# A two-block decoder on one core: the order of background steps on VectorE, ScalarE and GpSimd

## The chip, the core and the metric

The kernel runs on one core of one Trainium2 chip. The metric is the device time of one execution in microseconds; the median of three runs is given. The trace of one more execution on the same chip says what each engine did: TensorE (PE, with its weight loads PEld), VectorE (DVE), ScalarE (ACT), GpSimd (POOL) and SyncE (SP), whose queue issues nearly all DMAs.

## The reference

256 tokens of width 1024 pass through a first block of two layers and then a second block of one layer, all in float32. Cut to what matters:

```python
for l in range(2):
    x = x + 0.5 * swiglu(rms_norm(x, g1), w_gate, w_up, w_down)        # 1024 -> 2816 -> 1024
    pa, pb, pc, pd = split(rms_norm(x, gm) @ w_in)                     # 768, 416, 768, 512
    y = concat([neighbourhood(pa), mla(pb), differential(pc), gqa(pd)])
    x = x + y @ w_out
    x = x + 0.5 * swiglu(rms_norm(x, g2), ...)
    x = rms_norm(x, gf)
u = rms_norm(x) @ w_in_2                                               # second block
x = x + (ga * (pool(u) @ wa) + gb * (swa(u) @ wb) + gc * (moba(u) @ wc)) @ w_out_2
return rms_norm(x)
```

Each of the four mixers of a layer norms its heads (or its latents), forms scores, softmax and values for 256 queries and 256 keys, and norms its result. The weights are some 220 MB and are read once; the 256 tokens are two tiles of 128.

## The kernel before, in words

**Products.** A float32 product is made of three in the fast float32r form: every weight and every activation is held as a high part and a low part, and `acc` (line 339) adds high by high, high by low and low by high in PSUM. Activations are the stationary operand, weights the moving one, 512 columns wide.

**Weights.** `Weights` (from line 158) takes the weight matrices in one order, in units of 128 x 1024. `load` (line 183) starts the DMA of a unit into one of three staging buffers (`st`) from SP's queue. `cut` (line 194) makes the high part on ScalarE (`hi`, a copy to float32r) and the low part on VectorE (`lo`, a subtraction), into one of six pairs of buffers, and then starts the next load. A staging buffer is free when both have read it; a pair is free when the matmuls of its unit are done. `can_cut` (line 212) says whether the pair is free.

**Main line and background.** The main line is written out in order: gate, up and down products of a feed-forward net (`ffn`, line 546), the projections of the mixers (`proj`, line 496), the output projection (`wide`, line 521), and in the second block the same with gates. After each group of matmuls it calls `tick` (line 446), which resumes up to four background steps that are ready and emits one cut if it can. A background step is a Python generator put into a list by `spawn`: the chains of the four mixers (`differential` 928, `latent` 821 for the MLA heads, `neighbourhood` 960, `grouped` 977) with their head norms, `softmax_pv` (line 572, scores, softmax, transposes and values of one job after the other; one chain at a time may be in its scores) and the norm of the result (`post_rms`, line 765); in a feed-forward net the transposes of the hidden units (`trans_split`, line 394, spawned at line 562); at the start the second half of the first norm (lines 1093 to 1096); in the second block `moba` 1178, `swa` 1199, `pooling`, `silus` and `gated`. What is ready is decided by `Clock`, a small model of the engines' times that the kernel runs while it is traced. So the order of the program is this planner's. The main line's own work on other engines (evictions of a projection, updates of x, the norm of x between stages, the cuts) is not part of a step.

**From the program's order to the engines' queues.** The list scheduler of the language takes, for each engine, the instruction of lowest place among those that are ready; an instruction's place is its position in the program, counted over all engines. Every call on VectorE, ScalarE and GpSimd goes through `Engine` (line 125). There an instruction with an operand in PSUM is issued with `high_priority(14)`, which takes 14 off its place; others keep theirs. The two returns are the lines that the profile shows: L153 is an instruction issued ahead, L154 one that was not. TensorE's instructions (L333 matmuls, L337 transposes) and the DMAs always keep their places. Each engine then runs its queue in the order so found.

**Norms of heads.** `rpow` (line 348) makes the power -0.5 of several columns by a Newton iteration of eleven small instructions on VectorE (`ms`, `r`, then three times `q`, `q`, `r`), and of fewer than four columns by one instruction on GpSimd.

Of the kernel before, what the change touches and what calls it, by code (L numbers as in the profile page):

```python
# [39 lines left out]
FIRST = [1, 1, 2, 2, 2]  # L40
WARM = 6
AHEAD = 14
OUT_ORDER = (4, 5, 2, 3, 0, 1, 6, 7)
IN2 = {"ax": 0, "az": 512, "bq": 1024, "bkv": 1536, "bz": 1792,
       "cq": 2304, "ck": 2816, "cv": 3328, "cz": 3840, "g": 4352}
# [4 lines left out]
def _free(ap):  # L50
    n = 1
    for d in ap.shape[1:]:
        n *= d
    return n
# [6 lines left out]
class Clock:  # L61
# [3 lines left out]
    def __init__(self):  # L65
        self.t = {"pe": 0.0, "act": 0.0, "dve": 0.0, "pool": 0.0}
        self.last = 0.0
        self.writes, self.reads = {}, {}
        self.rings = {}

# [54 lines left out]
class Engine:  # L125
# [5 lines left out]
    def __getattr__(self, op):  # L131
        f = getattr(self._eng, op)

        def call(*args, **kw):
            aps = [v for v in list(args) + list(kw.values()) if isinstance(v, bass.AP)]
            outs = [kw["out"] if "out" in kw else args[0]]
            if "accum_out" in kw:
                outs.append(kw["accum_out"])
            ins = [v for v in aps if not any(v is o for o in outs)]
            n = max(_free(v) for v in [outs[0]] + ins[:1])  # L140
            sb = all(v.space != bass.MemoryType.PSUM for v in aps)
            if self.name == "act":
                cost = 55 + 0.84 * n + sum(93 for k in ("scale", "bias", "accum_out")
                                           if not isinstance(kw.get(k, 1.0), float))
            elif self.name == "dve":
                fast = sb and op in ("tensor_copy", "tensor_scalar")
                cost = 65 + (0.52 if fast else 1.04) * n
            else:
                cost = 300 + 165 * n if kw.get("op") == ALU.pow else 100 + 1.1 * n
            self._clock.op(self.name, cost, outs, ins)  # L150
            if not sb:
                with self._tc.high_priority(AHEAD):
                    return f(*args, **kw)  # L153
            return f(*args, **kw)  # L154
        return call
# [74 lines left out]
def decoder(ctx, tc, a, out):  # L230
    nc = tc.nc
    clock = Clock()
# [31 lines left out]
    for l in range(L):  # L264
        for f in (1, 2):
            if f == 2:
# [8 lines left out]
                ws.add(wi, 8, 512, 2, (OFF_GQA, OFF_GQA + 512))  # L275
                for k in OUT_ORDER:
                    ws.add(a["w_out"][l][k * 128:(k + 1) * 128, :], 1, D, 1)
# [143 lines left out]

    def resume(e):
        clock.last = e[2]
        try:
            d = next(e[0])
        except StopIteration:
            bg.remove(e)
            return
        e[2] = clock.last
        e[1] = d if callable(d) else clock.last if d is None else d  # L430

# [3 lines left out]
    def run_ready():  # L435
        for e in bg:
            if is_ready(e):
                resume(e)
                return True
        return False  # L440
# [12 lines left out]
    def drain_until(cond):  # L453

        while not cond():
            if not run_ready():
                e = min((e for e in bg if not callable(e[1])), key=lambda e: e[1])
                clock.wait_pe(e[1])
                resume(e)
# [61 lines left out]
    def wide(order, hi, lo, blocks, evac, before=None):  # L521


        nk = len(order)
        pss = [[psM() for _ in range(2)] for _ in range(2)]
        i0 = 0
        for b in blocks:
            w = [get() for _ in range(b)]
            last = i0 + b == nk
            for t in range(2):  # L530
                for hs in ((0,), (1,)) if last else ((0, 1),):
                    for i in range(i0, i0 + b):
                        k = order[i]
                        if before:
                            drain_until(lambda: before(k, t))
                        acc([(pss[t][h], h * 512, 512) for h in hs], hi[:, k, tok(t)],
                            lo[:, k, tok(t)], w[i - i0], 0, i == 0, i == nk - 1)
                        if t == 1 and hs[-1] == 1:
                            ws.end(w[i - i0])
                        if i < nk - 1:  # L540
                            tick()
                    if last:
                        evac(t, hs[0], pss[t][hs[0]])
            i0 += b
# [167 lines left out]
    def mixers(l, cols, rows, nlam, norm_out):  # L712
# [359 lines left out]
        def before(k, t):  # L1072
            k0 = k // 2 * 2
            return (k0, t) in finished and (k0 == 6 or (k0, 1) in finished)
        wide(OUT_ORDER, yTh, yTl, [1] * 4 + [4], lambda t, h, ps: norm_out.update(t, h, ps, 1.0),
             before)
# [367 lines left out]
```

## Time and profile before

| | |
|---|---|
| median of 3 runs | 1319.79 us (1315.48 to 1320.84) |
| the profiled execution | 1318.63 us |
| its span, first to last instruction | 1316.5 us |
| mean granted clock of TensorE | 0.995 |
| busy: PE, PEld | 98%, 79% |
| busy: DVE, ACT, POOL | 60%, 55%, 2% |

Times in the rows are microseconds, from the span's start. A matmul row counts as busy until its modelled end, and matmuls overlap; idle time stands in brackets behind a row with what ended it. The feed-forward nets and mixers follow one another: the first layer's mixers lie at about 205 to 345, the second layer's at about 715 to 865, the second block's attention at about 1085 to 1165.

### The profile page before, as it was taken

The page shows a single profiled execution, that of the slowest core. Times are in us where ns is not written, and L with a number is a line of the kernel's source. Part 1 is how long each engine was busy: PE and PEld are TensorE (multiplying, and loading weights), DVE is VectorE, ACT ScalarE, POOL GpSimd, SP SyncE. Part 2 cuts the span into 40 slices and gives each one's busy share as a digit, 9 for nine tenths or more (in the row PEclk, how much of TensorE's full clock was granted, in tenths as well). Part 3 has the DMA queues.
Part 4 walks back from the last instruction along what each step waited for, and adds up shares of the span by engine and source line. Part 5 has one row for each costly group of instructions (what it writes and reads, how often), then busy time and mean ns, then how long its engine had stood idle before and what let it go on. Part 6 is the DMA issues. An engine that isn't in the chain of part 4 may idle for free.

```text
span 1316.5 us, 17826 instructions
## 1 busy us (share of the span) xinstructions
PE 1291.3 (98%) x6514; PEld 1046.1 (79%) x6514; DVE 792.7 (60%) x1615; ACT 722.5 (55%) x1223; POOL 28.6 (2%) x44
## 2 busy tenths in 40 slices
PE   8999999999999999999999999999999999999997
PEld 7788888766788888788888876678888887678886
DVE  5655449895655544755545798565554565555475
ACT  6544437866644444644435676664444466566543
POOL 0000001000000000100000000000000000000000
PEclk9999999999999999999999998999999999999999
DMA  8766657432566665666665733156667474245652
GB/s 278 219 181 188 183 166 238 126 97 65 172 190 184 183 188 164 208 183 188 186 186 167 218 115 98 45 179 189 185 181 235 144 234 127 80 145 168 205 170 80
DMA packets 109815, 221.80 MB, mean 168 GB/s; under 512 B 7456, under 2 KB 30368, under 8 KB 109728
## 3 DMA queue, kind: packets, MB, share of 16 engines
q1 hardware_dynamic: 109152, 220.04, 55.5%
q8 instruction: 51, 0.84, 0.3%
q10 hardware_dynamic: 576, 0.63, 0.1%
q14 instruction: 36, 0.29, 0.1%
HBM read 219.59 MB, written 1.05 MB: 168 GB/s over the span
## 4 chain that ended last, share of the span: by engine, by line
PE 82%; DMA 6%; DVE 5%; ACT 4%; issue 1%; POOL 1%; SPq 0%; POOLq 0%; ACTq 0%; DVEq 0%
PE mmps L333 71%; PE tps L337 6%; PE sps L333 3%; DMA st<-in_w_in_dram 3%; PE tps L333 3%; DVE lo L154 2%; ACT hi L154 2%; DMA st<-in_ffn_w_gate_dram 2%; DMA st<-in_ffn_w_up_dram 1%; DVE xTl L153 1%; ACT junk L154 1%; ACT xTh L153 1%; POOL r L154 1%; DVE x L153 0%; DVE qkT L153 0%
## 5 line engine op out<-in xcount | busy, mean ns | idle before, releaser
L154 DVE TENSOR_TENSOR lo<-st,hi 128x1024 fp32r<-128x1024 f32 (+2 forms) x403 | 488.2, 1214 | 395.3 <-ACT hi L154 394.5
L154 ACT ACTIVATE hi<-st 128x1024 fp32r<-128x1024 f32 (+2 forms) x403 | 421.9, 1050 | 427.6 <-PE mmps L333 348.8
L333 PE MATMUL mmps<-hi,xTh 128*128 128x512 f32 (+2 forms) x1200 | 451.9, 377 | 1.0 <-ACT xTh L153 1.0
L333 PE MATMUL mmps<-hi,xTl 128*128 128x512 f32 (+2 forms) x1200 | 446.3, 372 | 0.0
L333 PE MATMUL mmps<-lo,xTh 128*128 128x512 f32 (+2 forms) x1200 | 446.2, 372 | 0.0
L333 PEld LDWEIGHTS mmps<-hi,xTh 128*128 128x128 f32 x1200 | 226.1, 188 | 42.4 <-issue 2.5
L333 PEld LDWEIGHTS mmps<-hi,xTl 128*128 128x128 f32 x1200 | 226.2, 188 | 38.2 <-issue 0.5
L333 PEld LDWEIGHTS mmps<-lo,xTh 128*128 128x128 f32 x1200 | 226.3, 189 | 36.2 <-issue 1.0
L333 PE MATMUL mmps<-lo,hTh 128*128 128x512 f32 x352 | 138.1, 392 | 0.0
L333 PE MATMUL mmps<-hi,hTh 128*128 128x512 f32 x352 | 137.8, 392 | 0.0
L333 PE MATMUL mmps<-hi,hTl 128*128 128x512 f32 x352 | 113.6, 389 | 0.0
L333 PE MATMUL mmps<-hi,yT 128*128 128x512 f32 (+1 forms) x248 | 89.0, 416 | 0.6 <-ACT yT L153 0.6
L333 PEld LDWEIGHTS mmps<-hi,hTl 128*128 128x128 f32 x352 | 66.1, 188 | 13.6
L333 PEld LDWEIGHTS mmps<-hi,hTh 128*128 128x128 f32 x352 | 66.1, 188 | 13.6
L333 PEld LDWEIGHTS mmps<-lo,hTh 128*128 128x128 f32 x352 | 66.1, 188 | 13.1
L154 POOL TENSOR_TENSOR r<-ms,mhalf 128x1 f32<-128x1 f32 x40 | 28.4, 711 | 1283.1 <-DVE ms L154 1283.0
L333 PEld LDWEIGHTS mmps<-hi,yT 128*128 128x128 f32 x248 | 46.1, 190 | 11.4 <-ACT yT L153 1.9
L333 PE MATMUL mmps<-lo,yT 128*128 128x512 f32 (+1 forms) x124 | 49.7, 401 | 0.0
L154 ACT ACTIVATE E<-E,nm 128x256 f32<-128x256 f32 (+1 forms) x80 | 38.3, 480 | 14.9 <-DVE nm L154 14.7
L153 ACT ACTIVATE fg<-mmps,r 128x512 f32<-128x512 f32 (+1 forms) x48 | 31.1, 652 | 21.7 <-PE mmps L333 21.7
L153 ACT ACTIVATE xTh<-tps,gains 128x128 fp32r<-128x128 f32 x112 | 31.6, 365 | 15.5 <-PE tps L337 15.5
L153 ACT ACTIVATE PT<-tps 128x512 f32<-128x512 f32 (+1 forms) x56 | 27.9, 502 | 21.4 <-PE tps L337 20.8
(172 smaller groups left out, 1035.0 us busy)
## 6 DMA issues: line engine op xcount, KB each, us to landing
st<-in_w_in_dram SPq DMA_DIRECT2D x90, 512.0 KB, 4.0
st<-in_ffn_w_up_dram SPq DMA_DIRECT2D x88, 512.0 KB, 4.0
st<-in_ffn_w_down_dram SPq DMA_DIRECT2D x88, 512.0 KB, 3.6
st<-in_ffn_w_gate_dram SPq DMA_DIRECT2D x87, 512.0 KB, 3.8
st<-in_w_out_dram SPq DMA_DIRECT2D x24, 512.0 KB, 3.7
st<-in_w_in_dram SPq DMA_DIRECT2D x8, 416.0 KB, 4.2
scratch<-in_t5b_dram SPq DMA_DIRECT2D x4, 512.0 KB, 5.1
scratch<-in_nab_dram SPq DMA_DIRECT2D x4, 512.0 KB, 7.3
```

The lines of the kernel that those rows point to most:

```text
L153: return f(*args, **kw)
L154: return f(*args, **kw)
L333: nc.tensor.matmul(ps, lhsT=lhsT, rhs=rhs, start=start, stop=stop)
L337: nc.tensor.transpose(ps, src, ident)
```

## The change

Every instruction that a background step issues on VectorE, ScalarE or GpSimd is issued with `high_priority(60)`, whether it has an operand in PSUM or not. Outside steps nothing changes: 14 with an operand in PSUM, 0 without. `resume` is the only function that runs a step.

```diff
 AHEAD = 14
+AHEAD_STEP = 60
...
         self.t = {"pe": 0.0, "act": 0.0, "dve": 0.0, "pool": 0.0}
         self.last = 0.0
+        self.in_step = False
...
             self._clock.op(self.name, cost, outs, ins)
-            if not sb:
-                with self._tc.high_priority(AHEAD):
+            if self._clock.in_step or not sb:
+                with self._tc.high_priority(AHEAD_STEP if self._clock.in_step else AHEAD):
                     return f(*args, **kw)
             return f(*args, **kw)
...
     def resume(e):
         clock.last = e[2]
+        clock.in_step = True
         try:
             d = next(e[0])
         except StopIteration:
             bg.remove(e)
             return
+        finally:
+            clock.in_step = False
```

## Rows read from the trace of the kernel before

**Rows 1.** The page: span, then busy us (share) and count by engine.

```profile
span 1316.5 us, 17826 instructions
PE 1291.3 (98%) x6514; PEld 1046.1 (79%) x6514; DVE 792.7 (60%) x1615; ACT 722.5 (55%) x1223; POOL 28.6 (2%) x44
```

**Rows 2.** Stretches: length, then PE, PEld, DVE, ACT, POOL busy, clock, DMA, GB/s.

```profile
40.00:60.00 20.00, 18.23 (x84) 14.73 (x83) 12.28 (x13) 10.71 (x12) 0.00 (x0) 1.00 0.76 232
260.00:280.00 20.00, 20.00 (x110) 15.80 (x109) 17.97 (x69) 11.83 (x23) 0.00 (x0) 1.00 0.58 173
280.00:300.00 20.00, 17.73 (x99) 12.16 (x98) 18.55 (x90) 12.52 (x35) 0.55 (x1) 0.91 0.12 39
380.00:400.00 20.00, 20.00 (x94) 16.53 (x93) 10.79 (x11) 9.84 (x11) 0.00 (x0) 1.00 0.65 195
740.00:760.00 20.00, 18.14 (x115) 14.65 (x114) 15.52 (x47) 16.13 (x41) 2.16 (x4) 1.00 0.65 197
1120.00:1140.00 20.00, 19.93 (x111) 13.43 (x110) 9.64 (x46) 13.55 (x41) 0.00 (x0) 1.00 0.33 93
```

**Rows 3.** The same view in stretches of 4 us, in both mixers.

```profile
280.00:284.00 4.00, 2.89 (x13) 1.73 (x11) 4.00 (x19) 3.23 (x10) 0.00 (x0) 1.00 0.16 60
284.00:288.00 4.00, 3.30 (x13) 2.78 (x13) 3.38 (x20) 2.63 (x9) 0.00 (x0) 0.67 0.00 0
288.00:292.00 4.00, 4.00 (x27) 2.56 (x27) 3.64 (x25) 2.58 (x8) 0.00 (x0) 0.90 0.00 0
...
800.00:804.00 4.00, 2.88 (x13) 1.72 (x11) 4.00 (x19) 3.23 (x10) 0.00 (x0) 1.00 0.12 47
804.00:808.00 4.00, 3.32 (x11) 2.85 (x12) 3.00 (x19) 2.12 (x8) 0.00 (x0) 0.53 0.00 0
808.00:812.00 4.00, 4.00 (x18) 2.51 (x16) 3.43 (x24) 1.89 (x6) 0.00 (x0) 0.62 0.00 0
```

**Rows 4.** Timeline of the last differential job: start, us, engine, line, output and inputs.

```profile
266.98 1.23 DVE L154 TENSOR_TENSOR lo<-st,hi 128x1024 fp32r<-128x1024 f32 x1
...
268.19 0.17 DVE L154 TENSOR_SCALAR nm<-mx 128x2 f32<-128x2 f32 x1
...
268.40 0.51 ACT L154 ACTIVATE E<-E,nm 128x256 f32<-128x256 f32 x1 [3.11 <-DVE nm L154]
...
269.61 1.20 DVE L154 TENSOR_TENSOR lo<-st,hi 128x1024 fp32r<-128x1024 f32 x1
...
271.01 1.22 DVE L154 TENSOR_TENSOR lo<-st,hi 128x1024 fp32r<-128x1024 f32 x1
...
272.23 0.48 DVE L154 SCALAR_TENSOR_TENSOR E<-E,cf 128x256 f32<-128x256 f32 x1
```

**Rows 5.** Timeline: that result's Newton chain, its first and last, and the next projection matmul.

```profile
279.60 0.17 DVE L154 TENSOR_SCALAR ms<-hss 128x4 f32<-128x4 f32 x1
...
284.57 0.16 DVE L154 SCALAR_TENSOR_TENSOR r<-q,r 128x4 f32<-128x4 f32 x1
...
287.76 0.99 PE L333 MATMUL mmps<-hi,yT 128*128 128x512 f32 x1
```

**Rows 6.** Timeline before the first scores of the second layer.

```profile
745.45 1.05 ACT L154 ACTIVATE hi<-st 128x1024 fp32r<-128x1024 f32 x1
...
747.12 0.39 PE L333 MATMUL sps<-qkT 32*128 32x256 f32 x2 [1.86 <-ACT qkT L153]
```

**Rows 7.** Timeline of ScalarE at the start: a cut, and the first square of x.

```profile
9.36 1.06 ACT L154 ACTIVATE hi<-st 128x1024 fp32r<-128x1024 f32 x1 [1.33 <-DMA st<-in_ffn_w_gate_dram]
...
13.33 1.07 ACT L154 ACTIVATE junk<-x 128x1024 bf16<-128x1024 f32 x1
```

**Rows 8.** Timeline of a cut and its first matmul; SP's waits (us, times, longest).

```profile
223.06 1.22 DVE L154 TENSOR_TENSOR lo<-st,hi 128x1024 fp32r<-128x1024 f32 x1 [0.44 <-ACT hi L154]
...
227.50 0.50 PE L333 MATMUL mmps<-hi,xTh 128*128 128x512 f32 x1
...
SPq L187 <- DVE lo L154: 823.8, 335, 19.7
```

## The prediction

> **What bounds the kernel now.** I read the busy totals first, then the stretches, then the order of single instructions where TensorE is short of work. TensorE is busy 1291.3 of 1316.5 us [rows 1], so 25.2 us of its time are empty, and nothing on VectorE or ScalarE can count except through such empty time or through its clock. The stretches say where it lies [rows 2]. In a feed-forward stretch (380 to 400) TensorE has no gap and VectorE is busy 10.79 of 20 us; in the second block's attention (1120 to 1140) it lacks 0.07 us. In the mixer of the first layer VectorE is busy 17.97 and then 18.55 of 20 us, and in the second of these stretches TensorE falls to 17.73 us at a mean granted clock of 0.91. Finer stretches [rows 3] put that loss between 280 and 292, and, for the second layer, which has the same pattern, between 800 and 812. So the change can act in two mixers of some 140 us each, in the first 60 us, and nearly nowhere else.
>
> **Places in time.** The two mixer stretches hold 110 + 69 + 23 and 99 + 90 + 35 instructions of TensorE, VectorE and ScalarE in 40 us [rows 2], 10.7 per us. So 60 places are about 5.6 us of program there, and 14 are 1.3 us. That is an estimate, since the places are counted in the program and the instructions in the trace.
>
> **What is moved.** The line of a row tells its old offset: L153 was issued 14 ahead (one operand in PSUM), L154 was not. Within steps both now get 60. Three orders change. A step's instruction that works in SBUF alone (maxima's sign, exponentials, reciprocals, the Newton chain of a norm) gains 60 places on the cuts of weights (`hi` on ScalarE, `lo` on VectorE) and 46 on the main line's evictions. One that reads PSUM gains 46 on the cuts. And inside the steps the lead of PSUM readers over SBUF work is gone: all go by their place. Nothing is added or removed, no DMA is issued in a step, and GpSimd's small powers have that engine to themselves. TensorE's own instructions keep their places.
>
> **Term 1, the voids at 280 and 800.** They hold 1.11 + 0.70 us of empty TensorE in the first layer and 1.12 + 0.68 in the second, together 3.6 us [rows 3]. The granted clock adds to it: 0.67, 0.90, 0.53 and 0.62 mean that the array worked part of each stretch at the lower of its two levels (1.2 GHz), after the gaps had begun. The share missing times the busy time is 0.33 x 3.30 + 0.10 x 4.00 + 0.47 x 3.32 + 0.38 x 4.00 = 4.6 us. So 8.2 us at most. What is late there is the differential heads' end: the output projection's matmuls come back at 287.76 [rows 5], when its last heads are normed. Two delays stand in front of that. In its last job the maximum's sign waits behind a `lo` from 266.98 to 268.19, with ScalarE idle for 3.11 us until it comes; the next two links stand behind the `lo` at 269.61 and at 271.01, so the sum of the two maps starts at 272.23 [rows 4]. Those are three cuts of 1.23, 1.20 and 1.22 us, 3.65 us. Then the Newton chain of that norm, 11 instructions of 0.16 to 0.17 us, 1.9 us by itself, takes from 279.60 to 284.73 [rows 5]; 3.2 us of that went to other steps' evictions, which had 14 places on it. Both go with the change, 6.8 us, and the void before 287.76 is about as long. Some of it comes back as waits among the steps themselves, which compete for VectorE as before. Ends: 0 and -8.2 us; I take -6.5, nearer to the far end, because the two delays add up to nearly the whole void.
>
> **Term 2, the first scores.** In the second layer TensorE is empty for 1.86 us before the first scores [rows 6], for an eviction of the transposed heads that stands behind a `hi` of 1.05 us; that stretch is the 18.14 us of rows 2. The eviction would go first. Ends: 0 and -1.9; I take -1.0, the one cut.
>
> **Term 3, the start.** The two steps that square x for the first norm stand at 13.33 and after it, behind a `hi` for which ScalarE sat idle 1.33 us [rows 7]. The first of them (1.07 us) needs only x, and would fit into that idle time; the cuts after it, the loads that wait for their buffers, and the gap in 40 to 60 (1.77 us, rows 2) would shrink. If it lands ahead of the first evictions of x instead, TensorE starts by its length later. Ends: -1.8 and +1.1; I take -0.8.
>
> **Term 4, cuts that come later.** A cut that is passed holds its staging buffer, and the next load of weights is queued on SP behind it: SP waits 823.8 us for `lo`, 335 times [rows 8]. The cover is the cut's lead on its matmul. The shortest I found is the neighbourhood heads' first unit, cut from 223.06 to 224.28 and used at 227.50 [rows 8]: 3.2 us. One passing step costs 0.2 to 0.7 us there, a burst of them 1 to 3 us, inside that lead. Ends: 0 and, worked out as a rival below, +19; I take +0.5, nearer to no cost because VectorE still has 1.5 to 2 us in 20 free.
>
> **Nothing** is put down for feed-forward steps and the second block: TensorE's lack there is under 0.1 us in 20 [rows 2], and what hides a shift of 1.2 us is the queue of weights already cut. If that cover were gone, each late unit would cost its lateness.
>
> **Sum.** -6.5 - 1.0 - 0.8 + 0.5 = -7.8 us. The profiled execution took 1318.63 us (its span of 1316.5 and 2.1 around it), so it would come to 1310.8. It lies 1.2 us under the median of the runs, 1319.79; from there the sum gives 1312.0, which I predict. A measurement of this kernel tells about 0.5% from no change, 6.6 us, so the forecast lies just beyond that bound.
>
> **Rivals.** *The voids stay.* What stands in front of the norms at 280 is mostly other steps, all with the same 60 places, and VectorE is full for 4.00 of 4 us [rows 3]; the cut-induced delays may be taken up by the order in which TensorE's queue reaches the transposes. Then only terms 2 to 4 are left, or less: 1316 to 1321 us. For it speaks that TensorE is empty for under 2% in all. It is also the case in which the change hardly does what it says, where a step's instruction was not ready earlier than it ran; in [rows 4] it was. The Trainium skill's page "Perfetto Trace Analysis", section "Identifying Performance Opportunities", says that improving a kernel generally means improving its most-contended engine; by that rule a change that leaves TensorE's work alone gives 0 us. The trace agrees for feed-forward stretches and not for the 12 us at 280. Chance 0.34.
>
> *Late cuts, slower.* Four kinds of units at the head of each mixer are used soon after they are cut. If bursts of steps hold a cut for the full 5.6 us of its 60 places, it is 2.4 us later than a lead of 3.2 us allows; four units in two layers make 8 x 2.4 = 19 us, and half of that, if every other unit is hit, 10 us: 1329 us. It decides where a cut is held for more than 3.2 us. Against it: VectorE's free time there. For it: ScalarE already sat 3.11 us behind an instruction that was not ready [rows 4], and a step put ahead of a cut too soon does the same to the cut. The skill's "TensorE: Matmul & The Clock Gate", in the table that opens it, gives ScalarE and VectorE strictly first-in-first-out queues; by it such a blocked place costs all that stands behind. The trace agrees with 3.11 us. Chance 0.19.
>
> **How the numbers follow.** The forecast, faster by more than 6.6 us, has 0.47; the voids staying 0.34; late cuts 0.19. The range takes in all ends of gain that the rows name (8.2 + 1.9 + 1.8 and a little of what is lost elsewhere in the mixers: 1304) and, of the slow case, its half size: 1304 to 1329. The forecast alone would be 1304 to 1313.
>
> **What would show it.** Right: `lo` instructions no longer stand between the links of a softmax chain (none between sign and exponential), the Newton chain at the end of the differential heads takes 2 to 3 us, TensorE's busy time in both voids rises to near 4 of 4 us and the granted clock to 1.00; the wait of 3.11 us is gone. Wrong: the clock dips stay in place (second case), or TensorE waits for `hi` or `lo` in the first 40 us of a mixer and SP's waits move there (third case). The forecast falls too if the voids close and new ones open later in the same mixer, which would say that the whole chain of heads, and not its head start, sets the stage.

## The result, and the profile after

The changed kernel takes 1335.16 us (median of 6 runs, 1330.13 to 1338.41) against 1320.32 us of the kernel before on the same chip: ratio 1.0116, 95% interval 1.0095 to 1.0137. It is slower, by more than the 0.5% that a measurement can tell, where 1312 us and "faster" were forecast.

The profiled execution took 1330.13 us, the fastest of its runs; its span is 1328.3 us against 1316.5 [rows 1]. What follows accounts for these 11.8 us; the median lies some 5 us higher, which one profile cannot show. First the page after, span and busy times:

```profile
span 1328.3 us, 17818 instructions
PE 1298.9 (98%) x6514; PEld 1051.9 (79%) x6514; DVE 796.2 (60%) x1615; ACT 724.3 (55%) x1223; POOL 29.4 (2%) x44
```

TensorE's empty time went from 25.2 to 1328.3 - 1298.9 = 29.4 us, 4.2 more, and its busy time from 1291.3 to 1298.9, 7.6 more, for the same 6514 matmuls and transposes: most of that is array time at the lower clock, as the stretches show. They say where, after first (columns as in [rows 2]), and behind it the four of before that did not stand there:

```profile
0.00:20.00 20.00, 15.27 (x57) 11.46 (x58) 10.82 (x35) 12.02 (x27) 1.31 (x6) 0.83 0.81 277
40.00:60.00 20.00, 19.05 (x85) 15.43 (x83) 12.20 (x13) 11.69 (x13) 0.00 (x0) 1.00 0.76 233
280.00:300.00 20.00, 16.68 (x87) 11.52 (x85) 17.39 (x85) 10.89 (x29) 0.00 (x0) 0.83 0.19 56
300.00:320.00 20.00, 17.95 (x115) 12.73 (x116) 11.88 (x43) 13.37 (x44) 2.10 (x3) 1.00 0.18 54
740.00:760.00 20.00, 19.31 (x126) 17.55 (x125) 17.48 (x49) 16.50 (x36) 3.08 (x4) 1.00 0.71 209
800.00:820.00 20.00, 17.45 (x88) 12.43 (x89) 16.07 (x71) 13.31 (x32) 0.00 (x0) 0.83 0.32 99
820.00:840.00 20.00, 17.55 (x93) 12.18 (x92) 12.13 (x50) 9.87 (x33) 1.95 (x2) 0.83 0.18 54
```

```profile
0.00:20.00 20.00, 16.37 (x73) 12.77 (x74) 12.31 (x37) 14.41 (x30) 1.31 (x6) 1.00 0.87 303
...
300.00:320.00 20.00, 19.43 (x121) 13.41 (x121) 11.72 (x44) 14.64 (x47) 1.64 (x3) 1.00 0.25 72
...
800.00:820.00 20.00, 17.59 (x91) 12.09 (x89) 17.47 (x88) 12.37 (x35) 0.55 (x1) 0.83 0.10 30
820.00:840.00 20.00, 19.44 (x123) 13.54 (x123) 12.34 (x44) 13.49 (x44) 1.09 (x2) 1.00 0.22 62
```

Between 280 and 320 TensorE is empty for 3.32 + 2.05 = 5.37 us after and 2.27 + 0.57 = 2.84 before. Between 800 and 840 it is 2.55 + 2.45 = 5.00 after and 2.41 + 0.56 = 2.97 before. The clock adds, by the working of term 1, 0.17 x 16.68 - 0.09 x 17.73 = 1.2 us in the first and 0.17 x 17.55 = 3.0 us in the second, where the stretch from 820 had the full clock before; at the start it adds 0.17 x 15.27 = 2.6 us. The two dips of [rows 3] have not closed; each has a second void behind it, some 16 us later.

The same event can be looked up in both traces, and its delay is a ledger of the loss. At the end of the first feed-forward block (an update of x at 200.48 us before) the changed kernel is 2.9 us behind. At the first gate evictions after the first mixer (347.28 before) it is 7.4 behind, so this mixer cost 4.5. At the first projections of the second mixer, two feed-forward blocks later (724.28), it is 7.3 behind; after the second mixer (868.66) 12.4, so that one cost 5.1. In the second block (gate evictions at 1240.87) it is 11.9 behind. **By this pair of profiles the start costs 2.9, the mixers 9.6, the second block gives back some 0.5, and feed-forward work changes nothing.** A ledger compares one execution of each kernel, so it has a spread of its own: run e8 below, whose program up to the second block is that of the kernel before, reads 2.6 us for the start and -1.8 for the two mixers.

Then what TensorE waited for in the first mixer (205 to 355 us; us in total, times, longest), after and before:

```profile
PE sps L335 <- ACT E L155: 2.4, 2, 2.0
PE sps L335 <- DVE q L155: 2.1, 1, 2.1
```

```profile
PE sps L333 <- ACT E L153: 2.3, 4, 1.1
```

Two waits of 2 us are new, and the second mixer (715 to 880 us) has two of 2.0 us again. All are waits of score matmuls (`sps`) for the PSUM buffer of earlier scores. The first, by the timelines of TensorE, VectorE and ScalarE (start, us, then as in [rows 4]):

```profile
281.91 1.03 PE L335 MATMUL sps<-kT,qT 96*128 96x256 f32 x4
...
285.67 0.70 PE L335 MATMUL sps<-kT,qT 96*128 96x256 f32 x2 [2.05 <-DVE q L155]
```

```profile
281.61 1.21 DVE L156 TENSOR_TENSOR lo<-st,hi 128x1024 fp32r<-128x1024 f32 x1
282.74 0.16 DVE L155 TENSOR_SCALAR ms<-hss 128x4 f32<-128x4 f32 x1
282.81 0.47 DVE L155 SCALAR_TENSOR_TENSOR qkT<-tps,qcol,qkT 128x256 fp32r<-128x256 f32 x1
...
284.60 0.42 DVE L155 TENSOR_REDUCE nm<-sps 128x1 f32<-128x256 f32 x1
...
287.35 0.15 DVE L155 SCALAR_TENSOR_TENSOR r<-q,r 128x4 f32<-128x4 f32 x1
```

```profile
285.06 0.47 ACT L155 ACTIVATE E<-sps,nm 128x256 f32<-128x256 f32 x1 [0.90 <-DVE nm L155]
```

The scores of the latent heads start at 281.91, and their row maximum `nm` runs at 284.60, 2.7 us later. Ahead of it stand the rest of a cut (`lo` of 281.61), four evictions of other heads (`qkT`) and five links of the Newton chain among them. By their starts these take 0.8, 1.5 and 0.4 us of the 2.7. Only then can the exponential at 285.06 read the scores, and only then are there buffers for the next. Releasers are inferred, so the `q` named for 285.67 is the event seen last; the exponential's end is at the same point. Before, the same pair stood 0.65 us apart, with one eviction and two links between:

```profile
279.79 1.03 PE L333 MATMUL sps<-kT,qT 96*128 96x256 f32 x4
...
280.44 0.42 DVE L153 TENSOR_REDUCE nm<-sps 128x1 f32<-128x256 f32 x1
```

### The profile page after: what moved, and what is told of

It reads as the page before. It is cut to its first block, busy times and chain, and to the rows that moved or that the text cites. A ratio compares the mean times of both kernels' runs of the same rounds, so it can differ in the third digit from the quotient of the medians.

```text
span 1328.3 us, 17818 instructions
## 1 busy us (share of the span) xinstructions
PE 1298.9 (98%) x6514; PEld 1051.9 (79%) x6514; DVE 796.2 (60%) x1615; ACT 724.3 (55%) x1223; POOL 29.4 (2%) x44
## 4 chain that ended last, share of the span: by engine, by line
PE 86%; DVE 6%; DMA 4%; ACT 3%; issue 1%; POOL 0%; POOLq 0%; ACTq 0%; SPq 0%
PE mmps L335 74%; PE tps L339 6%; PE sps L335 3%; PE tps L335 3%; DVE lo L156 2%; ACT hi L156 1%; DMA st<-in_ffn_w_up_dram 1%; DMA st<-in_w_in_dram 1%; DMA st<-in_w_out_dram 1%; DMA st<-in_ffn_w_gate_dram 1%; DVE x L155 1%; DVE hss L155 0%; DVE xTl L155 0%; ACT xTh L155 0%; DMA x<-in_x_dram 0%
## 5 line engine op out<-in xcount | busy, mean ns | idle before, releaser
L335 PE MATMUL sps<-kT,qT 64*128 64x256 f32 (+2 forms) x144 | 34.3, 382 | 5.0 <-DVE q L155 4.1
```

The source lines that it names most:

```text
L335: nc.tensor.matmul(ps, lhsT=lhsT, rhs=rhs, start=start, stop=stop)
```

## The experiments

Two theories were set against each other. **A: lost lead.** Before, in a step, an instruction that reads PSUM (row maxima, exponentials, evictions) was issued 14 places ahead, and one on SBUF alone was not. With both at 60 that lead of 14 is gone, and maxima come late behind links, rotations and norms of other heads. A1 puts the harm on VectorE, A2 on ScalarE. **B: SBUF work ahead of cuts.** The steps' SBUF work, wherever it passes the cuts of the weights and the main line, is the harm, and it grows with the offset. **C**, formed later, is about the cuts and stands at its runs. All ratios are to the kernel before on the same chip, with 95% intervals; the last column is what the two mixers cost together by the ledger of the run's one profile:

| run | PSUM / SBUF offset in steps | ratio | mixers, us |
|---|---|---|---|
| the change | 60 / 60 | 1.0116 [1.0095, 1.0137] | 9.6 |
| e1 | 60 / 60, start as before | 1.0101 [1.0074, 1.0127] | 10.9 |
| e2 | 74 / 60 | 1.0025 [1.0008, 1.0041] | 2.5 |
| e3 | 60 / 0 | 1.0062 [1.0039, 1.0086] | 3.3 |
| e4 | 14 / 14 | 1.0090 [1.0063, 1.0117] | 11.9 |
| e5 | 74 / 60, start as before | 1.0011 [0.9995, 1.0027] | -1.4 |
| e6 | 74 on VectorE, else 60 / 60 | 1.0054 [1.0033, 1.0075] | -2.4 |
| e7 | 74 on ScalarE, else 60 / 60 | 1.0139 [1.0115, 1.0164] | 18.0 |
| e8 | 60 / 60 in the second block alone | 1.0005 [0.9990, 1.0020] | -1.8 |
| e9 | 314 / 300, start as before | 0.9994 [0.9976, 1.0011] | -2.4 |
| e10 | 14 / 0, `lo` cuts 60 later in mixers | 1.0105 [1.0081, 1.0128] | 11.6 |
| e11 | e5, `lo` cuts 60 later in mixers | 1.0013 [0.9996, 1.0029] | -2.7 |
| e12 | 14 / 0, but 14 / 14 on VectorE after the first feed-forward block | 1.0061 [1.0040, 1.0081] | 10.0 |

The last column parts the runs. Without a lead on VectorE (the change, e1, e4, e7, e12) the mixers cost 9.6 to 18.0 us; with it (e2, e3, e5, e6, e9, e11) between -2.7 and 3.3, where mixers left as they were (e8) read -1.8. Only e10, which moves the cuts, loses with the lead in place.

### The lead given back (e2), and no lead at another size (e4)

```diff
-            if self._clock.in_step or not sb:
-                with self._tc.high_priority(AHEAD_STEP if self._clock.in_step else AHEAD):
+            n_ahead = (74 if not sb else 60) if self._clock.in_step else 0 if sb else AHEAD
+            if n_ahead:
+                with self._tc.high_priority(n_ahead):
```

> The change, but the instructions of steps that read or write PSUM are at 74 and those on SBUF alone at 60, so that the lead of 14 between the two is as before. Theory A expects most of the 9.5 us of the two mixers back, with the start's 2.9 us left: ratio 1.001 to 1.005. Theory B expects nothing back, since the SBUF work stands as far ahead of the cuts as in the change: 1.009 to 1.013.

Measured 1.0025: most of the loss is gone, as A expected, though the SBUF work stands as far ahead of the cuts as in the change. By the ledger of its profile the start still costs 2.9, and the mixers 1.5 and 1.0 in place of 4.5 and 5.1. Neither wait of 2 us is left; the largest of TensorE in the first mixer is 0.9 us. In the timelines of TensorE and VectorE, scores at 284.06 and maximum at 285.68, the rest of a cut and two evictions stand between, in place of four, and no link of a Newton chain:

```profile
284.06 1.03 PE L336 MATMUL sps<-kT,qT 96*128 96x256 f32 x4
...
284.89 0.87 DVE L156 SCALAR_TENSOR_TENSOR qkT<-tps,qcol,qkT 128x256 fp32r<-128x256 f32 x2
285.68 0.41 DVE L156 TENSOR_REDUCE nm<-sps 128x1 f32<-128x256 f32 x1
```

The other run keeps the lead away and makes the offset small:

```diff
-AHEAD_STEP = 60
+AHEAD_STEP = 14
```

> All instructions of steps are at 14 in place of 60: inside the steps PSUM readers have no lead, and SBUF work of steps passes 14 places. Theory A expects the mixers' loss nearly whole, since no lead is no lead at either size: 1.006 to 1.012. Theory B expects a loss that goes with the size: 1.001 to 1.005.

Measured 1.0090, in the range of A and above that of B. The mixers are hurt by what is equal, not by what is large.

### Which engine (e6, e7)

```diff
-            n_ahead = (74 if not sb else 60) if self._clock.in_step else 0 if sb else AHEAD
+            n_ahead = ((74 if self.name == "dve" else 60) if not sb else 60) if self._clock.in_step else 0 if sb else AHEAD
```

(the first line is that of e2; e7 has "act" for "dve")

> The change, but VectorE's PSUM instructions in steps (the row maxima of the scores, half of the evictions) are at 74; ScalarE's and all SBUF work stay at 60. Theory A1 (the maxima come late on VectorE behind the links of the Newton chains: the waits of the scores for E of 2.0 and for q of 2.1 us begin there) expects most of what the full lead gave: ratio 1.002 to 1.006, and no wait of the score matmuls over 1.2 us. Theory A2 (the exponentials and evictions come late on ScalarE, behind squares and cuts) expects little: 1.008 to 1.012.

> The counterpart: ScalarE's PSUM instructions in steps at 74, VectorE's at 60 with the SBUF work. Theory A1 expects little back: 1.008 to 1.012. Theory A2 expects most back: 1.002 to 1.006.

Measured 1.0054 with the lead on VectorE alone and 1.0139 with it on ScalarE alone. The waits of TensorE in the first mixer agree, e6 first:

```profile
PE sps L336 <- DVE qkT L156: 1.3, 1, 1.3
PE sps L336 <- ACT E L156: 1.2, 2, 0.8
```

```profile
PE sps L336 <- DVE q L156: 2.4, 1, 2.4
PE sps L336 <- ACT E L156: 2.0, 1, 2.0
```

With ScalarE's lead alone both waits of 2 us stay; with VectorE's alone both go, though one of 1.3 us (1.5 in the second mixer), over the bound of 1.2 that was expected, is there instead. That is A1. Whether ScalarE's lead adds anything to VectorE's stays open: e6 came out above e2, but their intervals overlap, and the profile of e6, its fastest execution (1320.71 us against 1324.81 to 1329.38), has no loss in the mixers. By itself ScalarE's lead gains nothing; e7 came out above its range, and its interval overlaps that of the change, so whether it does harm stays open too.

### The converse (e12)

```diff
+            n_ahead = (14 if not sb else (14 if self.name == "dve" else 0)) if self._clock.in_step else 0 if sb else AHEAD
```

(and `in_step` is set only after the first feed-forward block)

> The converse: the kernel before, with one thing taken away. From the end of the first feed-forward block on, VectorE's SBUF work in steps is issued 14 places ahead, as its PSUM instructions in steps and on the main line already are, so that the maxima have no lead over the links; ScalarE, GpSimd and the start are as before. Theory A1 (the lost lead on VectorE is the cause in the mixers) expects the mixers' loss: ratio 1.005 to 1.012, and waits of the score matmuls of about 2 us. If it takes the size of 60, or ScalarE's squares ahead of its exponentials as well, 0.998 to 1.004.

Measured 1.0061: in the kernel before, taking the lead away on VectorE alone, with ScalarE, the start and the size of 14 as they were, brings a loss, and its profile has it in the mixers (0.6 us behind at the first mixer, 4.8 after it, 5.2 and 11.1 at the second). That this also puts SBUF work 14 places ahead of the cuts, level with the main line's evictions, is not what costs: e5 and e9 put it 60 and 300 ahead with the lead kept, and no loss can be measured. The wait for E of 2.0 us is back; that for q is not. Here the second kind of void can be read, by VectorE, ScalarE and TensorE:

```profile
291.17 1.13 PE L337 MATMUL sps<-kT,qT 96*128 96x256 f32 x4
...
293.41 1.03 DVE L157 TENSOR_TENSOR prt<-ug,scratch 128x64 f32<-128x64 f32 x8
...
294.90 0.62 DVE L157 TENSOR_TENSOR pr<-ug,prt 128x256 f32<-128x256 f32 x2
295.11 1.06 ACT L158 ACTIVATE hi<-st 128x1024 fp32r<-128x1024 f32 x1
295.63 0.75 DVE L157 TENSOR_REDUCE nm<-sps 128x1 f32<-128x256 f32 x2
...
296.47 0.45 ACT L157 ACTIVATE E<-sps,nm 128x256 f32<-128x256 f32 x1
...
297.07 0.62 PE L337 MATMUL sps<-qkT 64*128 64x256 f32 x3 [2.00 <-ACT E L157]
```

The scores of 291.17 wait for their maxima until 295.63, behind the rotation of another head's queries (`prt`, `ug`, `pr`, SBUF alone). ScalarE meanwhile is in the cut of 295.11 and, behind it, a square, so the exponential starts only at 296.47, and TensorE is empty for 2.00 us. The changed kernel has the same picture at 301.56, with the maxima at 298.55.

### Too much lead (e3)

```diff
-            n_ahead = (74 if not sb else 60) if self._clock.in_step else 0 if sb else AHEAD
+            n_ahead = (60 if not sb else 0) if self._clock.in_step else 0 if sb else AHEAD
```

> Only the PSUM readers and writers of the steps are at 60; their SBUF work is not issued ahead, as before. Both theories expect the loss gone: A because the lead within the steps is even larger than before, B because no SBUF work passes a cut. Ratio 0.996 to 1.003. A ratio above 1.006 speaks against both: then it is the evictions of the steps that, at 60, pass something they should not.

A miss for both theories: 1.0062. Its first mixer has a wait that neither the kernel before nor the change has, for maxima `mx`:

```profile
PE sps L336 <- DVE mx L156: 2.2, 2, 1.7
```

What held these maxima was not followed. By the ledger its mixers cost 3.3 us, against 2.5 in e2. Its start is 3.1 us behind, though both squares of x stand where they stood before; other kernels with the old order at the start lag as much (next section). So e3 loses against the kernel before and less than the change, but whether a lead of 60 is worse than one of 14 is not shown: the intervals of e2 and e3 overlap, and the two differ in the place of the SBUF work as well.

### The start (e1, e5) and the second block (e8)

```diff
+        self.steps_lead = False
...
-        clock.in_step = True
+        clock.in_step = clock.steps_lead
...
         ffn(Norm(gains[:, 3 * l + 1]), FIRST if l == 0 else None)
+        clock.steps_lead = True
```

> The change, but no step leads before the first feed-forward block has ended (until then its PSUM readers are at 14 and its SBUF work at 0, as before); everything later stays at 60. The later clock of the changed kernel stands 2.9 us behind at the first gate evictions. Theory A (inside the steps the lead of PSUM readers over SBUF work was lost; the start is a separate loss, in which two squares of x of 0.96 us each stand ahead of the evictions of x transposed and of the cuts) expects the start's 2.9 us back and the mixers' 9.5 us kept: ratio to the kernel before near 1.008 (1.007 to 1.010). Theory B (the SBUF work of the steps runs ahead of the cuts of the weights, everywhere) expects the same here.

> PSUM instructions of steps at 74, SBUF work at 60, and no step issued ahead of the old places before the first feed-forward block has ended. Theory A (the lost lead in the mixers, and apart from it the start, where the old order came 2.0 us sooner: 0.9 against 2.9 us behind) expects the kernel with the lead restored, 1.0025, less 2.0 us: ratio 0.999 to 1.002. Theory B' (what is left after the lead comes back is the SBUF work ahead of the cuts in the mixers, and the start's loss is taken up again by the clock and the cuts later) expects no gain over 1.0025: 1.002 to 1.005.

Measured 1.0101, just above A's range, and 1.0011, inside it. Each is lower than its partner with the changed start (1.0116, 1.0025) by 0.0014 or 0.0015, 1.9 us, but both pairs of intervals overlap, so that difference rests on the two pairs agreeing and on the trace. ScalarE's timeline at the start of the changed kernel:

```profile
5.87 1.06 ACT L155 ACTIVATE junk<-x 128x1024 bf16<-128x1024 f32 x1 [0.85 <-DMA x<-in_x_dram]
...
6.92 2.16 ACT L155 ACTIVATE xTh<-tps,gains 128x128 fp32r<-128x128 f32 x8
9.57 1.06 ACT L155 ACTIVATE junk<-x 128x1024 bf16<-128x1024 f32 x1 [0.48 <-ACT xTh L155]
...
10.62 0.61 ACT L156 ACTIVATE hi<-st 128x512 fp32r<-128x512 f32 x1
```

Both squares, which stood at 13.33 [rows 7] and behind it, now stand ahead: one before the first evictions of x, one before the second cut. TensorE's first 20 us fall from 16.37 to 15.27 us of work, and the granted clock from 1.00 to 0.83. In the eight profiles with the old order there (the kernel before, e1, e5, e8 to e12) the stretch has 15.7 to 17.1 us at 0.91 to 1.00, and at the end of the first feed-forward block the ledger reads 0 to 3.3 us, 1.2 in the mean. In the four with both squares ahead (the change, e2, e6, e7) it has 14.8 to 15.8 us at 0.74 to 0.83, and the ledger reads 2.9 to 4.9, 3.6 in the mean. So the start costs some 2 us, and the 2.9 of one profile holds some of the spread between executions.

For e8, the change from the end of the first block on:

```diff
     b1.close()
+    clock.steps_lead = True
```

> The change with its one offset of 60 (no lead inside the steps), but only from the end of the first block on; before that the old places. In the changed kernel the second block came out 0.4 us shorter. Theory A expects that the loss is all in the start and the mixers: ratio 0.997 to 1.002. If the offset costs something everywhere (theory B), 1.003 or more.

Measured 1.0005, inside A's range. The offset costs and brings nothing there that could be measured.

### The cuts that were to leave (e9, e10, e11)

**C:** the cuts between the links of the last differential job are where no other instruction was ready, so no offset moves them and removing them from there is worth little.

```diff
+            n_ahead = (314 if not sb else 300) if self._clock.in_step else 0 if sb else AHEAD
```

> As the kernel with the lead restored and the old start (74 and 60), with 314 and 300 in place of 74 and 60. Theory C (the cuts that stand between the links of the last differential job don't stand there because their place is earlier: they are put where no instruction of a step is ready yet, so no offset moves them) expects the time of that kernel, 0.999 to 1.003, and the low-half cuts of 1.2 us still between the links near 267 to 275 us. Rival: 60 places are too few to pass the cuts; at 300 they go, and the voids near 280 and 800 us shrink by several us: 0.993 to 0.997.

> The kernel before (no step issued ahead), but the low-half cuts on VectorE are put 60 places later while a mixer runs, so that they yield to everything else. This tries by itself what the prediction gave 6.5 us for: cuts that no longer stand ahead of the steps' work. If the cuts between the links cost what the prediction said, 0.993 to 0.997. Theory C, by which the links wait for TensorE and ScalarE and cuts fill idle time, expects 0.998 to 1.003. If the late cuts then hold TensorE's projections (waits of mmps for lo of over 1 us each), 1.003 or more.

> The kernel with the lead restored and the old start (74 and 60: 1.0011), and the low-half cuts 60 places later in the mixers, so that they stand behind the steps' work by 120. By the prediction's price of the cuts 0.992 to 0.997; by theory C 0.999 to 1.004.

The edit of e10 and e11 (in e10 the steps have no offset of their own, in e11 they are those of e5):

```diff
-            self.dve.tensor_tensor(out=lo, in0=w, in1=hi, op=ALU.subtract)
+            with self.dve._tc.high_priority(-60 if self.clock.in_mixer else 0):
+                self.dve.tensor_tensor(out=lo, in0=w, in1=hi, op=ALU.subtract)
```

An offset of 300 gives 0.9994, like 60 (e5). The cuts between the links, by VectorE's timeline of the changed kernel and of e9 (300):

```profile
266.90 1.23 DVE L156 TENSOR_TENSOR lo<-st,hi 128x1024 fp32r<-128x1024 f32 x1
...
268.72 1.24 DVE L156 TENSOR_TENSOR lo<-st,hi 128x1024 fp32r<-128x1024 f32 x1
...
270.89 1.22 DVE L156 TENSOR_TENSOR lo<-st,hi 128x1024 fp32r<-128x1024 f32 x1
```

```profile
268.74 1.22 DVE L158 TENSOR_TENSOR lo<-st,hi 128x1024 fp32r<-128x1024 f32 x1
...
270.60 1.22 DVE L158 TENSOR_TENSOR lo<-st,hi 128x1024 fp32r<-128x1024 f32 x1
...
272.76 1.22 DVE L158 TENSOR_TENSOR lo<-st,hi 128x1024 fp32r<-128x1024 f32 x1
```

All three are still there, at 60 and at 300, one ahead of the sign and two between it and the sum of the two maps, as in [rows 4]; e9 is 2 to 3 us behind as a whole by then. So far C holds: putting the steps ahead does not move them. Putting the cuts back as well does. In e11, by VectorE and TensorE:

```profile
264.94 0.16 DVE L158 TENSOR_SCALAR nm<-mx 128x2 f32<-128x2 f32 x1
265.01 1.22 DVE L159 TENSOR_TENSOR lo<-st,hi 128x1024 fp32r<-128x1024 f32 x1
...
267.43 0.48 DVE L158 SCALAR_TENSOR_TENSOR E<-E,cf 128x256 f32<-128x256 f32 x1
...
280.30 1.03 PE L339 MATMUL sps<-kT,qT 96*128 96x256 f32 x4
```

No cut stands ahead of the sign and one behind it; ScalarE waits 1.42 us for the sign in place of 3.11, and the sum starts at 267.43, 4.8 us sooner than in the kernel before. So an offset can move the cuts, and C's reason, that nothing else was ready there, is not shown. But the gain is lost again within 13 us: the latent heads' scores start at 280.30, against 279.79 before, and the run takes 1.0013. What e11 shows is that taking these cuts away from there is worth nothing.

e10 itself is 1.0105, in the third case's range, but not for its reason: no matmul in its mixers waits for a `lo`. Two of its cuts, by VectorE's timeline, stand in the stretch where VectorE was already full before (18.55 of 20 us, [rows 2]) and where the kernel before has none between 275.96 and 295.33, and TensorE falls to 16.62 us in 280 to 300, with waits for exponentials and evictions:

```profile
279.74 1.23 DVE L157 TENSOR_TENSOR lo<-st,hi 128x1024 fp32r<-128x1024 f32 x1 [1.04 <-ACT hi L157]
...
282.27 1.23 DVE L157 TENSOR_TENSOR lo<-st,hi 128x1024 fp32r<-128x1024 f32 x1
```

The same edit with the steps ahead (e11) costs nothing: 1.0013. Why the same edit costs 1% without the steps' offset and nothing with it was not taken further. No version found is faster than the kernel before; e5, e8, e9 and e11 cannot be told from it.

## Why the prediction was wrong

**What bounds the kernel** was read right: all that was lost, as far as the ledger tells, was lost in the first 60 us and in the two mixers.

**The step that failed** is in "What is moved": "inside the steps the lead of PSUM readers over SBUF work is gone: all go by their place". It was seen, and given no term; "some of it comes back as waits among the steps themselves" took 0.3 us off term 1. It is the largest effect of all: giving the lead back alone takes the mixers' loss from 9.6 to 2.5 us by the ledgers (e2; -1.4 in e5), and the ratio from 1.0116 to 1.0025. In "Places in time" 60 places were 5.6 us of program; what decides among the steps is the difference, and that went from 14 places, 1.3 us by the same estimate, to none.

**Term 1 (-6.5 us)** measured +9.6 with the effect above in it. Without it, +2.5 (e2) and -1.4 (e5) lie on both sides of nothing. Its first half, 3.65 us of three cuts between the links, did not happen: the cuts stand at 266.90, 268.72 and 270.89, and ScalarE idles 3.42 us in place of 3.11. Where most of them did go (e11), nothing was gained (TensorE has 16.64 us of work in 280 to 300 there), so the void at 280 did not hang on that chain as the term had it. Its second half did not happen either. The Newton chain takes from 282.74 to 287.50, 4.8 us in place of 5.1, not the 2 to 3 that were to be the sign. The 3.2 us were put down to other steps' evictions alone. In the trace of before, four evictions took 1.5 us between the links by their starts, and four row maxima 1.3; the maxima are what the next scores wait for. The projection's matmuls come back at 292.61 against 287.76, 4.9 us later, of which 2.9 were there from the start.

**Term 2 (-1.0)** had the right size in its place: TensorE's empty time in 740 to 760 falls from 1.86 to 0.69 us, and the ledger goes from 7.3 us behind at 729.72 to 6.2 at 756.82. But at 768.28 it is back at 7.4, so nothing of it was kept.

**Term 3 (-0.8, ends -1.8 and +1.1)** measured some +2, outside its ends. The gap in 40 to 60 did shrink, by 0.8 us, but it did so in e1 too, with the old order (19.04 us busy). And not one square, two went ahead, and neither into the 1.33 us of idle time: one is ahead of the first evictions of x, which was the bad end, and with them came the clock at 0.83, which the end did not count.

**Term 4 (+0.5) and the slow rival.** That rival had the right sign (1329 us against 1335.16) and the wrong mechanism. SP's wait for `lo` grows from 823.8 us [rows 8] to 888.2, but its waits for VectorE's other instructions shrink nearly as much, and all its waits together go from 1142 to 1151 us in a span 11.8 us longer, so no delay of the loads is shown. No projection of a mixer waits for a cut. The page's costliest groups, where the last entry is what ended most of the idle time before, have 0.5 us of waiting for `lo` in the whole run, in the first 20 us; then SP's waits:

```profile
L335 PE MATMUL mmps<-lo,xTh 128*128 128x512 f32 (+2 forms) x1200 | 446.9, 372 | 0.5 <-DVE lo L156 0.5
```

```profile
SPq L189 <- DVE lo L156: 888.2, 351, 18.9
```

The behaviour that the rival's last sentences rested on is the one that decided, at another place: a maximum comes 2.7 us after its scores start, behind a cut, four evictions and five links of its queue. The Trainium skill's "TensorE: Matmul & The Clock Gate", in the table that opens it, has these queues strictly first-in-first-out, and the 2.7 us agree.

**The voids-stay rival** named the cause in passing ("what stands in front of the norms is mostly other steps, all with the same 60 places") and took it for a gain that does not come, with no price on the other side. The Trainium skill's rule in "Perfetto Trace Analysis", section "Identifying Performance Opportunities", that improving a kernel generally means improving its most-contended engine, gave 0 us as the prediction read it, since TensorE's work is untouched; the measured 1.16% is against that reading. VectorE, 60% busy, cost 0.6% by its order alone (e12).

**Nothing for feed-forward and the second block** was right: -0.1 and some -0.5 us by the ledger, and 1.0005 in e8.

## What to carry to other kernels

Issue offsets act by their differences. When one class of work is moved ahead, write down which orders inside that class are levelled, and put a price on that first: here a lead of 14 places for what frees PSUM (maxima, exponentials, evictions) over what stays in SBUF was worth about 1%, and moving both classes together by 60 or 300 with the lead kept, and the start left alone, was worth nothing. Before pricing a delay in a chain, ask whether what waits at its end waits for that chain: in e11 it ended 4.8 us sooner, and the next scores did not.

## What the runs showed of the hardware that was not expected

A short void costs more than itself. Of the 11.8 us that the span grew, 4.2 are empty time and 7.6 are the same matmuls taking longer: in the changed kernel's stretches from 0, 280 and 820 the mean granted clock is 0.83, part of each at the lower level of 1.2 GHz, where the kernel before has 1.00, 0.91 and 1.00; in the last two a void of 2 us came first. Part of the 7.6 may be chance, since single executions of the kernel before have mean clocks from 0.988 to 0.997. The clock does not follow the empty time of a stretch alone: the one from 300 is empty for 2.05 us at a clock of 1.00, that from 820 for 2.45 us at 0.83.
